# Down-projection weight sums stored unsplit, and block products added to the residual in place

## The chip, the cores and the metric

The kernel runs on one core of one Trainium2 chip. The metric is the device time of one execution in microseconds (us), the median of several runs. TensorE (PE) multiplies, VectorE (DVE) and ScalarE (ACT) do elementwise work, GpSimd (POOL) helps a little, and SyncE (SP) issues nearly all DMAs. Each engine takes its own instructions in order: an instruction that waits holds up all that stand behind it on that engine.

## The reference

A trunk of two layers over 1024 prompt frames and 32 sample frames (1056 columns), width 1024, all in float32. Layer 0 mixes by retention, layer 1 by gated linear attention (GLA); each is followed by a ConvFFN.

```python
for i in range(DEPTH):
    h = rmsnorm(x, norm_mix[i])
    y, S = retention_mixer(h, ...) if i % 2 == 0 else gla_mixer(h, ...)
    x = x + y
    h = rmsnorm(x, norm_ffn[i])
    u = h @ w_up                        # 1024 -> 2 x 2816
    c = conv_b + sum of 3 shifted u * conv_w
    gate, val = jnp.split(c, 2, axis=-1)
    x = x + (jax.nn.silu(gate) * val) @ w_down      # 2816 -> 1024
return rmsnorm(x, norm_final)
```

## The kernel before

Activations lie transposed: a tile has 128 features as its partitions and up to 1056 frames along the free axis. Every float32 operand of a matmul is split into two parts, `hi` (a cast on ScalarE, line 104) and `lo = x - hi` (a subtraction on VectorE, also line 104, in `load_w`), and a product is three matmuls: hi by hi, hi by lo, lo by hi. The raw weights land in a ring of three tiles (`raw_tile`, tag `raw`), the split ones in a ring of ten (`w_tile`).

One layer runs: the mixer; `second`, which has the gate projection (`pg`), the output projection (`Down` as `d1`, tile `pd`), which writes the residual to the DRAM tensor `scr_x`; the up projection and convolution (`ffn_up`, tile `pu`), whose 22 result tiles go to `scr_h`; and the down projection, which is the subject here.

The down projection has 22 k-tiles of 128. The first 16 are done in **pieces** (`Pieces`): two groups p of 8 k-tiles. In each p, 4 pairs q of output tiles and 2 halves s of the columns make 16 **units** (p, q, s). A unit is a 2x2 block product done with seven products instead of eight (`seven`; numbers m are 1 to 7, each product is 12 matmuls of 264 columns), in three PSUM banks. VectorE puts the bank sums together (`put`, line 1148), ScalarE copies banks out (`snap`, line 1137). The seven products need sums of weights (here S and T for each pair) and sums of activations. The activation operands of one (p, s) are made by `operands` from two staging buffers: 7 splits (cast at line 1090, subtraction at 1091) and 4 subtractions (line 1095), eleven steps that are spread over the products by `step`. The half s = 1 uses the same two staging buffers as s = 0, so its load of `scr_h` (line 1081) waits until the steps of s = 0 are done.

I call the start of the pieces, where the first operands are made while the up projection ends, the **junction**, and the place where p goes from 0 to 1 and all operands are made anew the **changeover**. There is one of each in each layer.

The weight sums are made early, in the retention stage, where VectorE and ScalarE have time: `presplit` loads two weight tiles, forms S and T on VectorE (lines 296 to 299, 128x512 each), splits each into hi and lo (ScalarE line 302, VectorE line 305) and stores four tiles to `scr_w`. A head of retention has nine chunks m; four sums are made in each head. In the pieces, `weights` loads the four split tiles (`ws`) straight into the ring of split weights, along with the plain weight g (split by `load_w`) and v.

A finished unit is stored to a DRAM tensor of its own, `scr_c`, one plane for each p. The last 6 k-tiles are the **plain rest** (`Down.run`, three chunks of 384, 384 and 288 columns). Its first chunk loads the residual `xr` from `scr_x`, and `add_more` loads both planes of `scr_c` piece by piece through the raw ring (`cx`, line 955) and adds them to `xr` on VectorE (line 957). Its weights w_down are loaded through the same raw ring into tiles `kw` and `kh`, its activations come from `scr_h` into `hh` and `hl`.

A scheduler sets the order of instructions on each engine from the program order, the free buffers and its own costs. So an edit can move instructions that it does not name.

## Time and profile before

| | |
|---|---|
| median of 3 runs | 2930.09 us (2929.4 to 2930.63) |
| profiled execution | 2926.68 us, its span 2924.9 us |
| mean granted TensorE clock | 0.988 |
| busy: TensorE / weight load / VectorE / ScalarE / GpSimd | 97% / 93% / 69% / 43% / 12% |
| moved by DMA | 414.20 MB, mean 142 GB/s |
| HBM read / written | 287.52 MB / 123.32 MB |
| stages, from the span's start | retention to about 566 us; gate, output and up projection of layer 0 to about 1395; pieces to about 1575; plain rest to about 1655; GLA to about 1960; then layer 1 in the same order, its pieces from about 2650 to 2835, its rest to the end |

The profiled execution is 3.4 us below the median, and its span is 1.8 us shorter than its time. A row of a timeline gives start, duration, engine, line and operation; in square brackets stands how long the engine was idle before it and what ended that wait. A row of the waits gives engine and line that waited, what ended it, and then the total in us, the times, and the longest. In the names, `pu` and `pd` are PSUM tiles, `AR` is one large SBUF region that holds staging buffers, unit results and residual chunks, `XA` and `XB` hold split activations.

### The profile page before, as it was taken

The page shows a single profiled execution, that of the slowest core. Times are in us where ns is not written, and L with a number is a line of the kernel's source. Part 1 is how long each engine was busy: PE and PEld are TensorE (multiplying, and loading weights), DVE is VectorE, ACT ScalarE, POOL GpSimd, SP SyncE. Part 2 cuts the span into 40 slices and gives each one's busy share as a digit, 9 for nine tenths or more (in the row PEclk, how much of TensorE's full clock was granted, in tenths as well). Part 3 has the DMA queues.
Part 4 walks back from the last instruction along what each step waited for, and adds up shares of the span by engine and source line. Part 5 has one row for each costly group of instructions (what it writes and reads, how often), then busy time and mean ns, then how long its engine had stood idle before and what let it go on. Part 6 is the DMA issues. An engine that isn't in the chain of part 4 may idle for free.

```text
span 2924.9 us, 51579 instructions
## 1 busy us (share of the span) xinstructions
PE 2835.9 (97%) x20618; PEld 2729.1 (93%) x20618; DVE 2020.9 (69%) x3307; ACT 1256.0 (43%) x2255; POOL 351.9 (12%) x564
## 2 busy tenths in 40 slices
PE   8999999999999999999898999999998999998997
PEld 8788988899999999999898989999998999998997
DVE  7756665644478877777654877774498777777548
ACT  5434342422355444444332555553254444444323
POOL 3010201000000111111000132220011111111002
PEclk9999999999999999999999999999999999999998
DMA  5544534554656122222677601114642222226675
GB/s 180 180 146 139 182 133 145 178 174 164 217 182 213 65 82 96 74 82 88 232 246 231 203 21 50 50 43 151 217 149 73 73 103 76 78 78 230 233 246 162
DMA packets 204784, 414.20 MB, mean 142 GB/s; under 512 B 25056, under 2 KB 124512, under 8 KB 204544
## 3 DMA queue, kind: packets, MB, share of 16 engines
q1 hardware_dynamic: 204000, 410.32, 41.6%
q8 instruction: 161, 2.64, 0.4%
q14 instruction: 79, 0.65, 0.1%
q10 hardware_dynamic: 544, 0.59, 0.1%
HBM read 287.52 MB, written 123.32 MB: 140 GB/s over the span
## 4 chain that ended last, share of the span: by engine, by line
PE 78%; DVE 11%; DMA 5%; ACT 3%; issue 2%; POOL 1%; DVEq 0%; SPq 0%; ACTq 0%; POOLq 0%
PE pu L1048 12%; PE pu L1043 12%; PE pu L1047 12%; PE pg L124 3%; PE pg L125 3%; PE pg L126 3%; PE pj L124 3%; PE pj L125 3%; PE pj L126 3%; PE pd L966 2%; PE pd L967 2%; PE pd L965 2%; PE psv L233 2%; PE psv L231 2%; PE psv L232 2%
## 5 line engine op out<-in xcount | busy, mean ns | idle before, releaser
L104 DVE TENSOR_TENSOR wlo<-raw,whi 128x1024 fp32r<-128x1024 f32 x164 | 208.2, 1272 | 88.7 <-ACT whi L104 77.2
L104 ACT CAST whi<-raw 128x1024 fp32r<-128x1024 f32 x164 | 171.1, 1050 | 218.7 <-issue 75.9
L1222 ACT COPY AR<-pu 128x264 f32<-128x264 f32 x264 | 99.1, 375 | 309.9 <-PE pu L1048 307.2
L124 PE MATMUL pj<-XA,whi 128*128 128x384 f32 (+1 forms) x576 | 189.8, 329 | 9.9 <-ACT whi L104 7.7
L125 PE MATMUL pj<-XA,whi 128*128 128x384 f32 (+1 forms) x576 | 188.5, 327 | 0.0
L126 PE MATMUL pj<-XA,wlo 128*128 128x384 f32 (+1 forms) x576 | 187.5, 326 | 0.9 <-DVE wlo L104 0.9
L124 PE MATMUL pg<-XA,whi 128*128 128x352 f32 x576 | 186.0, 323 | 0.0
L125 PE MATMUL pg<-XA,whi 128*128 128x352 f32 x576 | 184.6, 320 | 0.0
L126 PE MATMUL pg<-XA,wlo 128*128 128x352 f32 x576 | 184.5, 320 | 0.0
L149 POOL TENSOR_TENSOR ss<-ss,sq 128x264 f32<-128x264 f32 (+2 forms) x48 | 53.1, 1106 | 963.0 <-ACT sq L138 961.5
L966 PE MATMUL pd<-XB,whi 128*128 128x264 f32 x576 | 165.3, 288 | 3.3 <-DVE XB L935 3.1
L1244 DVE SCALAR_TENSOR_TENSOR AR<-AR,cw 128x1058 f32<-128x1058 f32 x88 | 116.0, 1320 | 72.3 <-ACT AR L1243 72.2
L967 PE MATMUL pd<-XB,wlo 128*128 128x264 f32 x576 | 164.7, 287 | 0.0
L965 PE MATMUL pd<-XB,whi 128*128 128x264 f32 x576 | 161.1, 288 | 0.0
L1048 PE MATMUL pu<-XA,wgl 128*128 128x264 f32 x528 | 150.1, 284 | 0.0
L1043 PE MATMUL pu<-XA,wgh 128*128 128x264 f32 x528 | 149.4, 283 | 0.0
L1047 PE MATMUL pu<-XA,wgh 128*128 128x264 f32 x528 | 149.3, 283 | 0.0
L1218 DVE TENSOR_TENSOR AR<-AR,pu 128x264 f32<-128x264 f32 (+2 forms) x440 | 145.5, 371 | 1.1 <-PE pu L1048 1.1
L1241 POOL COPY cst<-AR 128x2 f32<-128x2 f32 x88 | 50.6, 575 | 619.2 <-DVE AR L1218 619.2
L1195 DVE TENSOR_TENSOR wtl<-rv,wth 128x1024 fp32r<-128x1024 f32 x44 | 53.9, 1225 | 98.3 <-ACT wth L1194 97.3
L1148 DVE TENSOR_TENSOR AR<-AR,pu 128x264 f32<-128x264 f32 x128 | 53.5, 426 | 98.4 <-PE pu L1048 48.1
L124 PEld LDWEIGHTS pj<-XA,whi 128*128 128x128 f32 x576 | 109.7, 190 | 10.8 <-ACT whi L104 7.7
(414 smaller groups left out, 10508.4 us busy)
## 6 DMA issues: line engine op xcount, KB each, us to landing
ws<-scr_w SPq DMA_DIRECT2D x64, 512.0 KB, 4.4
raw<-w_ro SPq DMA_DIRECT2D x55, 512.0 KB, 3.8
rg<-w_up SPq DMA_DIRECT2D x44, 512.0 KB, 3.5
rv<-w_up SPq DMA_DIRECT2D x44, 512.0 KB, 3.4
scr_h<-AR SPq DMA_DIRECT2D x44, 512.0 KB, 2.6
AR<-scr_h SPq DMA_DIRECT2D x16, 1056.0 KB, 5.9
scr_c<-AR SPq DMA_DIRECT2D x32, 528.0 KB, 4.4
scr_w<-sp SPq DMA_DIRECT2D x32, 512.0 KB, 2.6
```

The lines of the kernel that those rows point to most:

```text
L104: ins = S.copy(hi, raw), V.tensor_tensor(lo, raw, hi.bitcast(F32), op=ALU.subtract)
L124: PE.matmul(ps, hi[:, k], rh, start=kt == 0, stop=False)
L125: PE.matmul(ps, hi[:, k], xl[:, kt, c0:c0 + n], start=False, stop=False)
L126: mm = PE.matmul(ps, lo[:, k], rh, start=False, stop=kt == KT - 1)
L965: PE.matmul(o, w[0][:, k], h[0][:, :n], start=i == 0, stop=False)
L966: PE.matmul(o, w[0][:, k], h[1][:, :n], start=False, stop=False)
L967: self.last_mm = PE.matmul(o, w[1][:, k], h[0][:, :n], start=False, stop=i == nk - 1)
L1043: mm = PE.matmul(ps, wh[:, k], x[:, 0, kt], start=m in (1, 2, 4, 5) and kt == 0, stop=False, skip_group_check=True)
L1047: PE.matmul(ps, wh[:, k], x[:, 1, kt], start=False, stop=False, skip_group_check=True)
L1048: mm = PE.matmul(ps, wl[:, k], x[:, 0, kt], start=False, stop=kt == 3, skip_group_check=True)
L1218: V.tensor_tensor(u[:, d:d + n], t[:, o:o + n], b[:, o:o + n], op=op)
L1244: V.scalar_tensor_tensor(cj, uj[:, 1:T + 3], cw[:, nt, 1:2], cj, op0=ALU.mult, op1=ALU.add)
```

## The change

There are two parts.

1. `weight_sums_out` takes the place of `presplit`. It makes S and T by the same four VectorE instructions and stores them as they are: two stores instead of four, no split. It is called in chunks m = 1 to 4 of each head instead of 0, 2, 4 and 6. In the pieces, `weights` now loads S and T with `load_w`: through the raw ring, cast on ScalarE, subtraction on VectorE.
2. `scr_c` and `add_more` are gone. A unit loads its own part of the residual from `scr_x` when it starts (`home`, into one of two buffers `res`), adds it when its seventh product is in (line 1138 after), and stores the sum back to `scr_x`. The results of units have two buffers instead of four. The plain rest loads `xr` from `scr_x` alone.

```diff
-    def presplit(l, p, q, pl):
+    def weight_sums_out(l, p, q):
...
         V.tensor_tensor(rv[:, b], rv[:, b], rg[:, a], op=ALU.subtract)
-        for j, r in enumerate((rg, rv)):
-            h = pl.tile([P, D], F32R, tag="ph_", name=f"sp{i}_{j}", bufs=2)
-            S.copy(h, r)
-            nc.sync.dma_start(scr_w[l, p, q, 2 * j], h.bitcast(F32))
-            lo = r.bitcast(F32R)
-            V.tensor_tensor(lo, r, h.bitcast(F32), op=ALU.subtract)
-            nc.sync.dma_start(scr_w[l, p, q, 2 * j + 1], r)
+        nc.sync.dma_start(scr_w[l, p, q, 0], rg)
+        nc.sync.dma_start(scr_w[l, p, q, 1], rv)
...
-                if m % 2 == 0 and m < 8:
-                    j = 4 * h + m // 2
-                    presplit(j // 8, j // 4 % 2, j % 4, rp)
+                if 1 <= m <= 4:
+                    j = 4 * h + m - 1
+                    weight_sums_out(j // 8, j // 4 % 2, j % 4)
...
-                def add_more(j):
-                    for src in self.more:
-                        t = raw_tile(f"cx{uid()}")[:, :2 * n].rearrange("p (k t) -> p k t", k=2)
-                        nc.sync.dma_start(t, src[:, 2 * j:2 * j + 2, c0:c0 + n])
-                        a = xr[:, 2 * j:2 * j + 2]
-                        V.tensor_tensor(a, a, t, op=ALU.add)
...
-            self.out = [AR[:, o:o + 4 * TH] for o in (0, 4 * TH, 8288, 8288 + 4 * TH)]
+            self.out = [AR[:, o:o + 4 * TH] for o in (0, 4 * TH)]
+            self.res = [AR[:, o:o + 4 * TH] for o in (8288, 8288 + 4 * TH)]
...
             g = load_w(io["w_dn"][self.l, p, q])
-            sums = [w_tile(f"ws{uid()}") for _ in range(4)]
+            sh, sl = load_w(scr_w[self.l, p, q, 0])
+            th, tl = load_w(scr_w[self.l, p, q, 1])
...
-            nc.sync.dma_start(sums[0].bitcast(F32), scr_w[self.l, p, q, 0])
...
+            def home(u):
+                return scr_x[:, u[1]::NPAIR, 2 * u[2] * TH:2 * (u[2] + 1) * TH]
...
-                    C[u] = self.out[units.index(u) % 4].rearrange("p (j t) -> p j t", j=2)
-                c = C[u]
+                    j = units.index(u) % 2
+                    C[u] = [x[j].rearrange("p (j t) -> p j t", j=2) for x in (self.out, self.res)]
+                    nc.sync.dma_start(C[u][1], home(u))
+                c, r = C[u]
...
                 if m == 3:
-                    nc.sync.dma_start(scr_c[p, :, q::NPAIR, 2 * s * TH:2 * (s + 1) * TH], c)
+                    V.tensor_tensor(c, c, r, op=ALU.add)
+                    nc.sync.dma_start(home(u), c)
```

Three places show how the order moves. Line numbers differ by 5 to 15 between the two kernels; the suffix of a name is only its serial number.

VectorE in the first head of retention. `pg`, `pv` are the weight tiles of the sums, `sp` their hi part, `kl`, `pl`, `vl` are lo parts that TensorE needs at once. Before:

```order
L305 TENSOR_TENSOR pg_684<-pg_684,sp_0_692 128x1024
L305 TENSOR_TENSOR pv_685<-pv_685,sp_1_697 128x1024
L104 TENSOR_TENSOR wlo_681<-raw_678,whi_680 128x1024
L333 TENSOR_TENSOR tc_653<-pj_604,cos 128x2x288
L334 TENSOR_TENSOR ts_654<-pj_604,sin 128x2x288
L450 TENSOR_TENSOR pm_705<-pss_702,rmask 128x128
L469 SCALAR_TENSOR_TENSOR kl_715<-pk_711,rcol,kh_714 128x256
L457 TENSOR_TENSOR pl_708<-pm_705,ph_707 128x128
L296 TENSOR_TENSOR pv_865<-pv_865 128x512
L297 TENSOR_TENSOR pg_864<-pv_865,pg_864 128x512
L298 TENSOR_TENSOR pg_864<-pg_864 128x512
L497 SCALAR_TENSOR_TENSOR vl_744<-psv_718,rc,vh_743 128x512
```

And now:

```order
L104 TENSOR_TENSOR wlo_681<-raw_678,whi_680 128x1024
L327 TENSOR_TENSOR tc_653<-pj_604,cos 128x2x288
L328 TENSOR_TENSOR ts_654<-pj_604,sin 128x2x288
L444 TENSOR_TENSOR pm_687<-pss_684,rmask 128x128
L463 SCALAR_TENSOR_TENSOR kl_697<-pk_693,rcol,kh_696 128x256
L451 TENSOR_TENSOR pl_690<-pm_687,ph_689 128x128
L295 TENSOR_TENSOR pv_857<-pv_857 128x512
L296 TENSOR_TENSOR pg_856<-pv_857,pg_856 128x512
L297 TENSOR_TENSOR pg_856<-pg_856 128x512
L298 TENSOR_TENSOR pv_857<-pv_857,pg_856 128x512
L444 TENSOR_TENSOR pm_767<-pss_764,rmask 128x128
L491 SCALAR_TENSOR_TENSOR vl_726<-psv_700,rc,vh_725 128x512
```

The two splits of the first sum are gone; the second sum still stands ahead of `vl`, now with all four of its instructions.

SP where the pieces of layer 0 end and the plain rest begins. `scr_c<-AR` (now `scr_x<-AR`) is the store of a unit, `raw<-w_down` a weight of the rest, `AR<-scr_h` one of its activations, `cx<-scr_c` a load of `add_more`. Before:

```order
L1152 DMA scr_c<-AR_5364 256x1x528
L276 DMA dmask<-dmask 128x128
L277 DMA lmask<-lmask 128x256
L955 DMA cx_16005<-scr_c 128x2x384
L955 DMA cx_16040<-scr_c 128x2x384
L955 DMA cx_16043<-scr_c 128x2x384
L932 DMA AR_5364<-scr_h 128x384
L102 DMA raw_16071<-w_down 128x1024
L955 DMA cx_16080<-scr_c 128x2x384
L955 DMA cx_16083<-scr_c 128x2x384
L932 DMA AR_5364<-scr_h 128x384 x3
L102 DMA raw_16111<-w_down 128x1024
```

And now, from the store of the last unit but one; `AR<-scr_x 128x8x384` is the load of `xr`:

```order
L1139 DMA scr_x<-AR_5236 256x1x528
L102 DMA raw_15995<-w_down 128x1024
L273 DMA ba<-ba 128x4
L274 DMA smask<-smask 128x384
L275 DMA dmask<-dmask 128x128
L276 DMA lmask<-lmask 128x256
L1139 DMA scr_x<-AR_5236 256x1x528
L102 DMA raw_16029<-w_down 128x1024
L102 DMA raw_16063<-w_down 128x1024
L937 DMA AR_5236<-scr_x 128x8x384
L925 DMA AR_5236<-scr_h 128x384
L102 DMA raw_16098<-w_down 128x1024
```

The first weight that the rest loads for itself (raw_16071 before, raw_15995 now) has moved from behind the last unit's store and three loads of `cx` to ahead of that store; the load of `xr`, which before stood ahead of the last two stores, now stands behind the last one.

VectorE at the changeover of layer 0, from the first split for the half s = 0. `XA<-AR,XA` is such a split, `AR<-AR 128x1056` a subtraction of operands, `AR<-AR,pu` a `put`, `wlo` a lo part of a weight. Before:

```order
L1091 TENSOR_TENSOR XA<-AR_5364,XA 128x1056
L1148 TENSOR_TENSOR AR_5364<-AR_5364,pu_14887 128x264
L104 TENSOR_TENSOR wlo_14931<-raw_14928,whi_14930 128x1024
L1148 TENSOR_TENSOR AR_5364<-AR_5364,pu_14833 128x264
L1091 TENSOR_TENSOR XA<-AR_5364,XA 128x1056 x2
L1148 TENSOR_TENSOR AR_5364<-AR_5364,pu_14947 128x264
L1095 TENSOR_TENSOR AR_5364<-AR_5364 128x1056
L1148 TENSOR_TENSOR AR_5364<-AR_5364,pu_14887 128x264
L1095 TENSOR_TENSOR AR_5364<-AR_5364 128x1056
L1091 TENSOR_TENSOR XA<-AR_5364,XA 128x1056
L1148 TENSOR_TENSOR AR_5364<-AR_5364,pu_15001 128x264
L1091 TENSOR_TENSOR XA<-AR_5364,XA 128x1056
```

And now; line 1138 is the new addition of the residual, line 1080 the subtraction of operands:

```order
L1076 TENSOR_TENSOR XA<-AR_5236,XA 128x1056
L1134 TENSOR_TENSOR AR_5236<-AR_5236,pu_14787 128x264
L104 TENSOR_TENSOR wlo_14832<-raw_14829,whi_14831 128x1024
L1134 TENSOR_TENSOR AR_5236<-AR_5236,pu_14732 128x264
L1076 TENSOR_TENSOR XA<-AR_5236,XA 128x1056
L1138 TENSOR_TENSOR AR_5236<-AR_5236 128x1056
L1076 TENSOR_TENSOR XA<-AR_5236,XA 128x1056
L1134 TENSOR_TENSOR AR_5236<-AR_5236,pu_14852 128x264
L1080 TENSOR_TENSOR AR_5236<-AR_5236 128x1056
L1134 TENSOR_TENSOR AR_5236<-AR_5236,pu_14787 128x264
L1080 TENSOR_TENSOR AR_5236<-AR_5236 128x1056
L1076 TENSOR_TENSOR XA<-AR_5236,XA 128x1056
```

From the first to the last of the seven splits and three subtractions of this half (some rows go on below these) there stood six `put` and one `wlo` among them; now there are eight `put`, three `wlo`, one lo part of v (128x512) and two additions. On SP the loads of `scr_h` into the two staging buffers for s = 1 had one load of `ws` between them; now the store of a unit stands there, which waits for that unit's addition on VectorE.

More of the change, by code (lines that the diff above doesn't have):

```diff
@@ L256, in trunk_kernel @@
     scr_w = io["scr_w"]
-    scr_c = io["scr_c"]
     ident = cp.tile([P, P], F32, tag="ident", name="ident")
@@ L901, in trunk_kernel, with __init__ @@
     class Down:
-        def __init__(self, nk, wsrc, hsrc, chunks, res, sm, keep, hold, more=()):
+        def __init__(self, nk, wsrc, hsrc, chunks, res, sm, keep, hold):
             self.nk, self.wsrc, self.hsrc, self.chunks, self.res, self.sm = nk, wsrc, hsrc, chunks, res, sm
-            self.more = more
             self.hw = max(n for _, n in chunks)
@@ L970, in run @@
                     self.load(c, kt)
-                    if self.more and i < 4:
-                        add_more(i)
                     if c == len(self.chunks) - 1 and i == nk - 3:
@@ L1103, in weights @@
             g = load_w(io["w_dn"][self.l, p, q])
-            sums = [w_tile(f"ws{uid()}") for _ in range(4)]
+            sh, sl = load_w(scr_w[self.l, p, q, 0])
+            th, tl = load_w(scr_w[self.l, p, q, 1])
             v, rv = w_tile(f"wv{uid()}"), raw_tile(f"rv{uid()}")
-            nc.sync.dma_start(sums[0].bitcast(F32), scr_w[self.l, p, q, 0])
-            nc.sync.dma_start(sums[1].bitcast(F32), scr_w[self.l, p, q, 1])
-            nc.sync.dma_start(sums[2].bitcast(F32), scr_w[self.l, p, q, 2])
-            nc.sync.dma_start(sums[3].bitcast(F32), scr_w[self.l, p, q, 3])
             nc.sync.dma_start(rv[:, b], io["w_dn"][self.l, p, q + NPAIR][:, b])
@@ L1112, in weights @@
             V.tensor_tensor(v[:, b], rv[:, b], v[:, a].bitcast(F32), op=ALU.subtract)
-            sh, sl, th, tl = sums
             self.W[p, q] = {1: (g[0][:, a], g[1][:, a]), 2: (g[0][:, b], g[1][:, b]),
@@ L1328, in second @@
         down = Down(NF - NS, lambda k: io["w_down"][l, k], lambda k: scr_h[NS + k], CM, scr_x, sm,
-                    range(NF - NS), 3, (scr_c[0], scr_c[1]))
+                    range(NF - NS), 3)
         with pool(f"xb{l}") as xbp:
@@ L1560 @@
 _SCRATCH = {"scr_or": (16, P, T), "scr_og": (8, P, T), "scr_h": (NF, P, T), "scr_x": (P, KT, T),
-            "scr_w": (2, 2, NPAIR, 4, P, D), "scr_c": (2, P, KT, T)}
+            "scr_w": (2, 2, NPAIR, 2, P, D)}
 def kernel(**inputs):
```

## The prediction

> **What bounds the kernel now.** I read the page first: TensorE is the bound, and it is nearly full.
>
> ```profile
> span 2924.9 us, 51579 instructions
> PE 2835.9 (97%) x20618; PEld 2729.1 (93%) x20618; DVE 2020.9 (69%) x3307; ACT 1256.0 (43%) x2255; POOL 351.9 (12%) x564
> ```
>
> No matmul is removed, so only TensorE's idle time (89 us in all) and the slow matmuls after a wait can be won. Next I read the busy time by stretch: two of retention, the junction of layer 0 (1395 to 1425), its changeover (1471 to 1512) and the start of its plain rest (1573 to 1606); layer 1 looks alike.
>
> ```profile
> core 0: us, PE busy (x) PEld busy (x) DVE busy (x) ACT busy (x) POOL busy (x), PEclk, DMA share, GB/s
> 60.00:195.00 135.00, 131.45 (x692) 114.29 (x691) 91.96 (x164) 55.24 (x93) 16.33 (x13) 0.99 0.44 153
> 195.00:325.00 130.00, 127.71 (x674) 110.35 (x674) 84.58 (x154) 52.53 (x90) 13.80 (x11) 1.00 0.45 155
> ...
> 1395.00:1425.00 30.00, 22.11 (x141) 20.87 (x140) 29.16 (x32) 16.19 (x18) 4.69 (x4) 0.83 0.58 196
> 1471.00:1512.00 41.00, 40.07 (x327) 39.63 (x326) 33.03 (x39) 20.43 (x29) 0.00 (x0) 1.00 0.65 219
> 1573.00:1606.00 33.00, 25.07 (x130) 23.36 (x129) 18.91 (x27) 9.47 (x15) 0.00 (x0) 0.90 0.82 259
> ```
>
> Two things are to be seen. TensorE idles where the change takes work away (3.6 and 2.3 us in retention, 7.9 us at the start of the rest). And the change puts work onto VectorE where VectorE is fullest: 29.2 of 30 us at the junction, 33 of 41 at the changeover, where TensorE now hardly waits. ScalarE is at half there, so casts that move to it hide.
>
> **Retention: minus 5.** What TensorE waits for from 60 to 566 us, from the groups by line:
>
> ```profile
> L513 PE MATMUL po<-vl,ph 128*128 128x512 f32 x32 | 13.5, 420 | 5.1 <-DVE vl L497 5.1
> L511 PE MATMUL po<-vh,ph 128*128 128x512 f32 x32 | 13.0, 406 | 2.3 <-ACT vh L496 2.1
> ```
>
> The largest of these, from the timeline: VectorE stands at the second weight sum until its load is in, and `vl` is queued behind it.
>
> ```profile
> 78.86 0.69 DVE L296 TENSOR_TENSOR pv<-pv 128x512 f32<-128x512 f32 x1 [3.58 <-DMA pv<-w_dn]
> ...
> 81.72 0.79 PE L513 MATMUL po<-vl,ph 128*128 128x512 f32 x1 [3.43 <-DVE vl L497]
> ```
>
> The load waits for a raw tile, and that for the stores of the first sum. These stores now start when the sums are made, not after the splits; what leaves that chain, per sum:
>
> ```profile
> L302 ACT CAST sp<-pg x16: 1039/1051/1057, 64.7 to 530.0; 128x1024 fp32r<-128x1024 f32 x16
> L305 DVE TENSOR_TENSOR pg<-pg,sp x16: 1209/1220/1226, 67.8 to 534.1; 128x1024 fp32r<-128x1024 f32 x16
> ```
>
> Two subtractions of 1.22 us (second row) and a cast of 1.05 make 3.5 us, as much as the wait of 3.43 us. Against that one more 0.69-us instruction of the second sum now stands ahead of `vl`. So this wait shrinks by about 2.8 us. Of the other 4.0 us (7.4 minus 3.43) I take 2.2: half of them end on ScalarE, which no longer casts sums. Bounds: minus 7.4 if all go; plus 3.4 if the sums, now one in each of four neighbouring chunks, make that wait once more.
>
> **Sums in the pieces: minus 2.9.** TensorE's waits in the pieces of layer 0, then of layer 1:
>
> ```profile
> PE pu L1043 <- ACT XA L1090: 3.9, 1, 3.9
> PE pu L1043 <- ACT AR L1137: 2.8, 1, 2.8
> PE pu L1048 <- DMA ws<-scr_w: 1.8, 3, 0.9
> ...
> PE pu L1043 <- DMA ws<-scr_w: 0.3, 1, 0.3
> ```
>
> ```profile
> PE pu L1048 <- DMA ws<-scr_w: 0.8, 2, 0.5
> ```
>
> The last three rows go: 1.8 + 0.3 + 0.8 = 2.9 us. The load waited for a split tile to come free and then took its landing; now the raw tile is loaded ahead, and after the release only a cast and a subtraction are left (1.05 + 1.22 us), so I keep all of it. Bounds: 0 to minus 2.9.
>
> **Plain rest: minus 12.** In layer 0 TensorE waits three times for `kw`, 7.9 us in sum (first row), and the first wait leaves it slow (the rows below).
>
> ```profile
> PE pd L965 <- ACT kw L104: 7.9, 3, 5.0
> ```
>
> ```profile
> 1582.83 0.33 PE L966 MATMUL pd<-hs,whi 128*128 128x384 f32 x1
> 1583.00 0.34 PE L967 MATMUL pd<-hs,wlo 128*128 128x384 f32 x1
> 1588.30 0.69 PE L965 MATMUL pd<-hh,kw 128*128 128x384 f32 x1 [4.96 <-ACT kw L104]
> ...
> 1593.24 0.38 PE L967 MATMUL pd<-hh,kw 128*128 128x384 f32 x1
> ```
>
> Starts are 0.17 us apart before the wait; after it 14 matmuls take 4.9 us instead of 2.4, which is 2.5 us more. The cause is on SP, in program order:
>
> ```profile
> 1576.11 0.53 SPq L1152 DMA_DIRECT2D scr_c<-AR  x1
> ...
> 1578.29 1.45 SPq L955 DMA_DIRECT2D cx<-scr_c  x3
> ...
> 1582.91 0.34 SPq L102 DMA_DIRECT2D raw<-w_down  x1
> ```
>
> The weight is issued at 1582.9, behind `cx` loads that hold the raw ring. Now its load stands ahead of the last unit's store at 1576, and two more follow that store at once; it is there some 7 us earlier, over the 5.0 us that it was late. So 7.9 + 2.5 = 10.4 us are at stake; I take 9.5, since the fourth weight now stands behind the load of `xr`. What is late next is `xr` itself, which waits for the store of the last unit. Landing times, medians:
>
> ```profile
> scr_c<-AR SPq DMA_DIRECT2D x32, 528.0 KB, 4.4
> ...
> AR<-scr_x SPq DMA_DIRECT2D x4, 1536.0 KB, 7.1
> ```
>
> With the new addition (1.25 us, below) that store is issued at about 1577.4, `xr` at 1582 and landed at 1589. A k-tile is 24 matmuls at 0.17 us, 4.1 us; two of them end at 1583.2, so the chunk begins at 1575, and its first result is evicted once five are through: 1596. So 7 us of slack, and the load is hidden. Layer 1 has these waits in its rest:
>
> ```profile
> PE pd L965 <- DVE rm L207: 1.9, 1, 1.9
> ...
> PE pd L965 <- ACT kw L104: 0.8, 1, 0.8
> PE pd L967 <- DVE kw L104: 0.6, 1, 0.6
> ```
>
> `kw` is earlier in the same way, and `rm` is VectorE's norm behind the additions of `add_more`. Of 3.3 us I take 2.5. Bounds for both rests: 0 to minus 13.7.
>
> **VectorE in the pieces: plus 11.** Each of the 32 units gets an addition of 128x1056, and each of the 16 weight pairs two subtractions of 128x1024. The operand subtraction has the addition's shape; the `cx` additions that go are the second row.
>
> ```profile
> L1095 DVE TENSOR_TENSOR AR<-AR x8: 1250/1253/1260, 1391.7 to 1422.7; 128x1056 f32<-128x1056 f32 x8
> ```
>
> ```profile
> L957 DVE TENSOR_TENSOR AR<-AR,cx x48: 695/951/1768, 1576.8 to 2901.6; 128x768 f32<-128x768 f32 x32, 128x576 f32<-128x576 f32 x16
> ```
>
> So the pieces gain 32 x 1.25 + 32 x 1.22 = 79 us of VectorE, the rests lose about 46, retention 39. Inside a p, a pair lasts 20 us and VectorE is mostly free: nothing on the path. At a changeover it is. Four units in 41 us bring 4 x 1.25 + 4 x 1.22 = 9.9 us to the 33.0 already there: 42.9 in 41, so at least 1.9 us is late. In the order, the operands of s = 0 now have two `wlo`, two additions, a lo part of 128x512 (0.7 us, as the instruction of that shape at 78.86) and two `put` more among them (264 columns, a quarter of the addition's, so 0.3 us or more each): 2.4 + 2.5 + 0.7 + 0.6 = 6.2 us. They themselves have time, but the staging buffers come free later, and with them the operands of s = 1, which have none:
>
> ```profile
> 1488.29 0.77 SPq L1081 DMA_DIRECT2D AR<-scr_h  x1
> ...
> 1497.92 1.26 DVE L1095 TENSOR_TENSOR AR<-AR 128x1056 f32<-128x1056 f32 x1 [1.46 <-DMA AR<-scr_h]
> ...
> 1500.92 0.28 PE L1043 MATMUL pu<-XA,whi 128*128 128x264 f32 x1
> ```
>
> The load lands 9 us after its issue; three microseconds later TensorE uses the first operand made of it. A delay of 6.2 us, less the 1.5 us of VectorE's wait that fill, would leave 4.7 us on TensorE. Products of later units, which the order now pulls forward there, take part of it; a wait of this size also slows the matmuls behind it. I take 5 for each changeover, 10 in all. Bounds for each: 0 and 9.9. At the junction the first operands have one `wlo` more and one less ahead of their last split, so I take 0.5 each, with bounds of minus 2.8 (its `snap` wait gone) and plus 4.
>
> On slowing, the junction: after a wait of 2.78 us a matmul takes 0.42 us instead of 0.28.
>
> ```profile
> 1402.95 0.28 PE L1048 MATMUL pu<-XA,ws 128*128 128x264 f32 x1
> 1406.01 0.59 PE L1043 MATMUL pu<-XA,ws 128*128 128x264 f32 x1 [2.78 <-ACT AR L1137]
> 1406.39 0.42 PE L1047 MATMUL pu<-XA,ws 128*128 128x264 f32 x1
> ```
>
> The Trainium skill ("TensorE: Matmul & The Clock Gate", What's actually happening) lets the clock fall only after an idle window of about 3.4 us. By that rule changeover waits of 2 to 3 us would cost their own length alone, an estimated 2 us less in all, and the sum would be minus 11; the row above shows slow matmuls after less, and I go by it.
>
> SP issues 80 fewer DMAs, and `scr_w` moves 16.8 MB less each way; no queue is the bound, so no time is booked. The ScalarE casts (32 x 1.05 us) leave retention and hide in the pieces.
>
> **Sum.** Minus 5, 2.9, 9.5 and 2.5, plus 10 and 1: minus 8.9 us. The profiled execution took 2926.68, so 2917.8; the median shown is 3.4 us above it: 2930.09 - 8.9 = 2921.2. I predict 2921 us.
>
> **Rivals.**
> - *VectorE takes it all back.* At junction and changeover the new subtractions stand ahead of the operand splits in full: 9.9 us for each changeover, 4 for each junction, 28 us against gains of 20: plus 8, 2938 us. It decides against the change once the four places cost over 6.5 us each on average. For it: 29 of 30 us busy, and the load behind a unit's store. Against it: TensorE's order has other products there. Chance 0.20 (slower 0.12, the same 0.08).
> - *The rest only changes its wait.* The load of `xr` and what stands behind it on SP are late, as when the chain store, load takes its slow cases, and 8 of the 12 us stay: minus 1, 2929 us. For it: the DMA share of 0.82 there. Against it: 7 us of slack. Chance 0.10 (the same 0.08, slower 0.02).
> - *The changeovers cost nothing.* Products of the next pair fill every hole, or the loads land sooner: minus 18 to minus 20, 2911 us. For it: the same scheduler's order at this changeover leaves TensorE 0.9 us idle of 41 today. Against it: 42.9 us of VectorE work in 41. The Trainium skill ("DMA: Bandwidth & Descriptors", Anatomy of one DMA) fits a transfer that GpSimd issues as 2.0 us plus its bytes over 436 GB/s; for the 1.08 MB of a staging load this is an estimated 4.5 us, and s = 1 would be 4 us earlier than I reckon, which is this case; the trace's 9 us speaks against it. Chance 0.22, faster.
>
> **How the numbers follow.** The forecast, minus 3 to minus 14 us, has 0.48 (faster 0.37, the same 0.11). 0.2% is 5.9 us, about what a measurement of this kernel can tell from no change. Sums: faster 0.37 + 0.22 = 0.59; the same 0.11 + 0.08 + 0.08 = 0.27; slower 0.14. The range runs from the full gain at 2908 (all waits of 21 to 24 us gone) to 2934, halfway into the first rival; the forecast's own is 2916 to 2927.
>
> **What would show it.** Retention: the wait for `vl` near 80 us under 1 us. Pieces: no wait for a sum's DMA; new waits of PE for XA or XB near the changeovers, 3 to 6 us each, with VectorE full. Rest: no `kw` wait near 1585, PE's chunk begun without a hole, `xr` landed 5 us or more before its first use. Wrong would be: a long wait of PE for `xr`'s eviction, or changeovers without a hole.

## The result and the profile after

| | before | after |
|---|---|---|
| median (4 runs each) | 2930.36 us (2929.4 to 2932.72) | 2905.28 us (2904.3 to 2905.55) |
| profiled execution, its span | 2926.68 us, 2924.9 us | 2905.39 us, 2903.6 us |
| ratio | | 0.9913, 95% interval 0.9895 to 0.993 |

The change makes the kernel 25 us faster by the medians and 21.3 us by the two profiled spans. The difference of 3.8 us is in the execution that was profiled before, 3.7 us below its median. The step-by-step comparison goes by the spans. Measured once more (e9 below) the same kernel gave 0.9928 (0.9906 to 0.9951). The forecast was minus 8.9 us; 2905 lies 2.7 us under the range. First the page of after:

```profile
span 2903.6 us, 51344 instructions
PE 2824.7 (97%) x20618; PEld 2721.1 (94%) x20618; DVE 2019.9 (70%) x3291; ACT 1254.2 (43%) x2255; POOL 350.7 (12%) x564
```

VectorE's total is the same within 1 us: its work has moved, and has not become less. The busy time by stretch, with the columns of before: two stretches of retention, then junction, changeover and start of the rest in layer 0. The last three begin 8 or 9 us earlier than the stretches of before, as the whole stage does.

```profile
60.00:195.00 135.00, 134.88 (x720) 118.46 (x719) 84.04 (x155) 46.04 (x83) 16.61 (x14) 1.00 0.41 137
195.00:325.00 130.00, 129.01 (x684) 111.97 (x683) 79.11 (x150) 46.04 (x83) 11.89 (x11) 1.00 0.35 117
1386.00:1416.00 30.00, 21.24 (x142) 19.84 (x141) 29.26 (x31) 17.41 (x21) 6.00 (x4) 0.83 0.60 191
1463.00:1504.00 41.00, 39.23 (x314) 38.22 (x313) 36.18 (x42) 20.75 (x29) 0.00 (x0) 1.00 0.62 209
1565.00:1598.00 33.00, 29.57 (x172) 28.51 (x171) 19.72 (x32) 16.16 (x29) 1.65 (x2) 1.00 0.88 304
```

Retention is nearly full, the rest has gained 4.5 us in 33 at full clock, the changeover has lost 0.8 us and the junction 0.9. TensorE's waits in retention and in the pieces of layer 0:

```profile
PE po L507 <- DVE vl L491: 0.9, 1, 0.9
```

```profile
PE pu L1027 <- ACT XA L1075: 6.4, 1, 6.4
PE pu L1027 <- ACT XB L1075: 2.1, 3, 1.2
PE pu L1027 <- ACT AR L1121: 1.0, 1, 1.0
PE pu L1027 <- DVE AR L1205: 0.6, 1, 0.6
PE pu L1031 <- DVE XA L1076: 0.4, 1, 0.4
```

Of 7.4 us of waits in retention 0.9 is left. No wait for a sum's load is left in the pieces. The junction has one wait of 6.4 us and a shorter one where it had 2.8 and 3.9. The changeover has 1.7 us, two of the three in the second row.

The next table has the length of each stage in us, from TensorE's first matmul of that stage to that of the next, read from the timeline. "Again" is the second profile of the changed kernel; e1 and e2 are the two parts of the change alone (below).

| stage | forecast change | before | after | again | e1 sums | e2 residual |
|---|---|---|---|---|---|---|
| start, to retention's first state product | 0 | 70.5 | 69.3 | 69.0 | 68.9 | 68.6 |
| retention | -5 | 508.4 | 499.8 | 499.8 | 500.6 | 507.5 |
| gate projection 0 | 0 | 171.8 | 171.8 | 171.8 | 171.8 | 171.8 |
| output projection 0 | 0 | 190.2 | 191.3 | 190.9 | 190.5 | 190.1 |
| up projection and pieces 0 | +3.4 | 634.1 | 635.3 | 634.1 | 633.0 | 631.8 |
| plain rest 0 | -9.5 | 97.8 | 89.4 | 89.2 | 95.1 | 90.8 |
| GLA | 0 | 320.2 | 320.1 | 320.2 | 321.2 | 320.1 |
| gate and output projection 1 | 0 | 197.9 | 197.9 | 196.3 | 198.3 | 197.0 |
| up projection and pieces 1 | +4.7 | 640.4 | 642.4 | 640.5 | 639.8 | 638.5 |
| plain rest 1, to the end | -2.5 | 93.6 | 86.4 | 86.3 | 92.9 | 86.3 |

(The forecast's sums in pieces, changeover and junction are put together per layer: -2.1 + 5 + 0.5 and -0.8 + 5 + 0.5.) Between two executions of the changed kernel a stage moves by up to 2 us, so only the retention, the rests and, by its waits, the changeover can be read one by one. In the nine other runs below whose edits leave retention as in the change it takes 499.7 to 504.3 us (e5 is the longest), and 508.4 and 507.5 where it is as before: its gain is clear, but a difference of less than 5 us in that stage is not.

The first chunk of layer 0's rest, from the timeline (SP's load of `xr`, VectorE's first eviction, TensorE's two waits):

```profile
1573.64 0.58 SPq L937 DMA_DIRECT2D AR<-scr_x  x1
...
1588.87 1.59 DVE L1393 TENSOR_TENSOR AR<-AR,pd 128x384 f32<-128x384 f32 x3 [2.27 <-PE pd L953]
...
1596.26 0.91 PE L951 MATMUL pd<-hh,whi 128*128 128x384 f32 x2 [2.92 <-DVE AR L1393]
1597.65 0.45 PE L952 MATMUL pd<-hl,whi 128*128 128x384 f32 x1 [0.49 <-DVE hl L928]
```

The eviction waited for TensorE and not for `xr`, whose load is issued 15 us earlier. TensorE's waits for `kw` are gone; what is late next is the eviction itself, 3.4 us at the chunk's end (the last two rows).

Layer 1's rest, its second half and its tail, by stretch, before and then after:

```profile
2869.00:2907.60 38.60, 36.74 (x232) 35.76 (x230) 33.85 (x49) 12.82 (x28) 4.43 (x5) 0.96 0.53 167
...
2907.60:2924.90 17.30, 4.45 (x11) 2.18 (x10) 8.86 (x13) 5.94 (x16) 4.26 (x4) 0.59 0.29 102
```

```profile
2853.40:2888.00 34.60, 34.51 (x229) 33.74 (x228) 27.73 (x40) 12.38 (x28) 4.68 (x5) 1.00 0.38 128
2888.00:2903.60 15.60, 3.23 (x10) 1.65 (x10) 8.31 (x12) 5.38 (x14) 3.94 (x4) 0.73 0.28 100
```

About the same matmuls take 34.6 us instead of 38.6, at a clock of 1.00 instead of 0.96, and the tail is some 1.6 us shorter.

### The profile page after: what moved, and what is told of

It reads as the page before. It is cut to its first block, busy times and chain, and to the rows that moved or that the text cites. A ratio compares the mean times of both kernels' runs of the same rounds, so it can differ in the third digit from the quotient of the medians.

```text
span 2903.6 us, 51344 instructions
## 1 busy us (share of the span) xinstructions
PE 2824.7 (97%) x20618; PEld 2721.1 (94%) x20618; DVE 2019.9 (70%) x3291; ACT 1254.2 (43%) x2255; POOL 350.7 (12%) x564
## 4 chain that ended last, share of the span: by engine, by line
PE 85%; DVE 8%; DMA 2%; ACT 2%; issue 1%; POOL 1%; SPq 0%; DVEq 0%; ACTq 0%; POOLq 0%
PE pu L1032 13%; PE pu L1027 13%; PE pu L1031 13%; PE pd L952 3%; PE pd L953 3%; PE pd L951 3%; PE pg L124 3%; PE pg L125 3%; PE pg L126 3%; PE pj L125 3%; PE pj L124 3%; PE pj L126 3%; PE psv L233 2%; PE psv L231 2%; PE psv L232 2%
## 5 line engine op out<-in xcount | busy, mean ns | idle before, releaser
L104 DVE TENSOR_TENSOR wlo<-raw,whi 128x1024 fp32r<-128x1024 f32 x196 | 246.3, 1259 | 126.3 <-ACT whi L104 76.3
L104 ACT CAST whi<-raw 128x1024 fp32r<-128x1024 f32 x196 | 204.3, 1048 | 286.4 <-PE pj L125 91.8
L1027 PE MATMUL pu<-XA,whi 128*128 128x264 f32 x448 | 129.3, 289 | 15.4 <-ACT XA L1075 13.5
L1031 PE MATMUL pu<-XA,whi 128*128 128x264 f32 x448 | 128.5, 288 | 0.7 <-DVE XA L1076 0.7
L1032 PE MATMUL pu<-XA,wlo 128*128 128x264 f32 x448 | 127.9, 288 | 0.0
```

What stands on the lines that cost most here:

```text
L104: ins = S.copy(hi, raw), V.tensor_tensor(lo, raw, hi.bitcast(F32), op=ALU.subtract)
L1027: mm = PE.matmul(ps, wh[:, k], x[:, 0, kt], start=m in (1, 2, 4, 5) and kt == 0, stop=False, skip_group_check=True)
L1031: PE.matmul(ps, wh[:, k], x[:, 1, kt], start=False, stop=False, skip_group_check=True)
L1032: mm = PE.matmul(ps, wl[:, k], x[:, 0, kt], start=False, stop=kt == 3, skip_group_check=True)
```

## The experiments

**The two parts alone: e1 and e2.** e1 has the hunks of `weight_sums_out` and of `weights` only, e2 those of `Pieces.run` and `add_more` only.

> The first part of the change alone: weight sums unsplit in DRAM and split on load; the units still go to their own scratch and the plain rest still adds them there. Theory A (the two parts act in separate stages): only the retention gain of 8.6 us and the 1.2 us of the start come, the pieces stay within 2 us, and the rests keep their waits for kw: about 2930 - 10 = 2920 us. Rival B (the rest's gain comes from the lighter loads of sums ahead of it, not from the cx loads that are gone): the rest of layer 0 loses most of its 7.9 us wait for kw here too, 2912 us or less.

> The second part alone: units add to the residual in place, sums still split in retention and kept as four halves. Theory A: the rests give what they gave in the whole change (8.5 and 7.2 us), the retention nothing, and the addition costs the pieces 0 to 2 us: 2930 - 15 = 2915 us. Rival B: the rests keep half of the waits and the time is 2922 us or more. The two single parts should add up: e1's and e2's gains together 25 us within 3 if A holds.

Measured: e1 0.9972 (0.9963 to 0.9981), e2 0.9945 (0.9929 to 0.9962). The reductions of 0.28% and 0.55% add up to the change's 0.72 to 0.87%. By the table e1 brings the retention and leaves the rests, e2 brings the rests and leaves the retention. TensorE's longest wait in layer 0's rest, in e1 and in e2:

```profile
PE pd L960 <- ACT kw L104: 6.3, 2, 4.7
```

```profile
PE pd L956 <- DVE AR L1402: 2.9, 1, 2.9
```

Theory A holds: the parts act in separate stages. e1's rest 0 is 2.7 us shorter than before, so a little of rival B is there. In the pieces each part alone is faster than both together, by 1 to 4 us; by the stage spread this is not sure, but the waits at the changeover go the same way: 1.0 and 1.1 us (layers 0 and 1) in e1, which has the new subtractions of weights alone, none in e2, which has the additions alone, 1.7 in both layers with the two together.

**More VectorE work in the pieces: e3, e4, e13, e14, e15.** All add additions on a residual tile that is no longer needed, so the output stays; they differ in where. The five edits in one, the conditions in words:

```diff
                     V.tensor_tensor(c, c, r, op=ALU.add)
                     nc.sync.dma_start(home(u), c)
+                    for _ in range(k):      # e3: 1, e4: 3, for every unit
+                        V.tensor_tensor(r, r, c, op=ALU.add)
+                    # e13: 2 if q in (1, 2); e14: 4 if q == 1; e15: 1 for the
+                    # units (0,2,1), (0,3,0), (0,3,1), (1,0,0); otherwise 0
```

> The changed kernel with one more VectorE addition of 128x1056 (1.25 us) per unit, on the residual tile behind the store: the output is not touched. Theory A (the prediction's: VectorE is on the path at junction and changeover): four more of them at each changeover are 5 us, of which 4 show, and about 1 at each junction: plus 8 to 12 us, 2915 us. Theory B (the changeover's end is set by when the staging loads of s = 1 land, and VectorE waits there): plus 0 to 2 us, 2906 us.

> The same with three more additions per unit, 15 us of VectorE at each changeover, where the changed kernel leaves VectorE 4.8 us idle of 41. Theory A: plus 24 to 36 us, 2935 us. Theory B: the idle 4.8 us fill and the rest shows: plus 10 at each changeover, 2925 us; if products of later units cover more, plus 5 in all.

> The changed kernel with as many extra VectorE additions as e3 (32 of 128x1056), but two each at the units of the second and third weight pair of a part, none at the first and fourth: none at the junction and the changeover. Theory A (inside a part VectorE's work is off the path, only the changeover counts): no wait at the changeover beyond the 1.7 us of the change, plus 0 to 1 us on it, 0.9925. Theory B (any added VectorE work in the pieces costs, wherever it stands): as e3, plus 9 us, 0.996.

> The changed kernel with 32 extra VectorE additions of 128x1056 as in e3, but four each at the units of the second weight pair of a part, at least 20 us away from the changeover on either side (in e13 the last two extras of the third pair still fell into the changeover, at 1467.6 and 1469.1 us). Theory A (VectorE's work costs only where the operands of the next part are made): the waits of the changeover stay at 1.7 us, plus 0 to 2 us on the changed kernel (0.9913 to 0.9935). Theory B (work anywhere in the pieces costs, since it queues ahead of the operands): 3 us or more for each changeover, plus 6 to 9 us, 0.9955.

> The changed kernel with only 8 extra additions, one each at the four units that end in each changeover. Theory A: almost all of e3's price, 4 to 5 us for each changeover, plus 8 to 10 us, 0.9955. Theory B: a quarter of e3's price, plus 2 to 3 us, 0.9935.

| run | extra additions, where | ratio (interval) | changeover waits of TensorE, layers 0 / 1 | up projection and pieces 0 / 1 |
|---|---|---|---|---|
| after, again | 0 | 0.9928 (0.9906 to 0.9951) | 1.8 / 1.7 us | 634.1 / 640.5 us |
| e14 | 32, second pair | 0.9935 (0.992 to 0.995) | 1.7 / 2.7 | 634.5 / 643.0 |
| e13 | 32, second and third pair | 0.9951 (0.9937 to 0.9964) | 4.2 / 3.9 | 637.8 / 645.3 |
| e15 | 8, changeover only | 0.997 (0.9958 to 0.9983) | 5.6 / 5.0 | 641.1 / 646.0 |
| e3 | 32, one per unit | 0.997 (0.9957 to 0.9983) | 5.0 / 5.4 | 640.5 / 646.7 |
| e4 | 96, three per unit | 1.0009 (1.0 to 1.0019) | 7.6 / 7.6 | 643.8 / 650.5 |

Eight additions at the changeovers cost as much as thirty-two spread over all units, and thirty-two away from them cost nothing that can be told. So within the pieces VectorE's added work is on the path at the changeover: theory A of e14 and e15. e3 came out as its theory A, with 5.2 and 4.2 us on the pieces. e4's pieces are 8.5 and 8.1 us longer than those of the change, nearer to its theory B (10 for each changeover) than to A; another 6.8 us came in layer 0's rest and 2.7 in GLA, which neither theory had. e13, meant to show this first, did not: two of its additions still fell into the changeover, and the expectation of 0 to 1 us was wrong. TensorE's waits at layer 0's changeover in e14, then in e15:

```profile
PE pu L1027 <- ACT XB L1075: 1.7, 2, 1.3
```

```profile
PE pu L1027 <- ACT XA L1075: 4.3, 1, 4.3
PE pu L1027 <- ACT XB L1075: 0.8, 2, 0.4
PE pu L1027 <- DVE AR L1134: 0.5, 1, 0.5
```

Why does the change itself not pay this price? The staging loads of s = 1 and the casts of what they bring, in the timeline of after, then of e15, then of e2:

```profile
1483.15 0.37 SPq L1066 DMA_DIRECT2D AR<-scr_h  x1
1488.54 0.60 SPq L1066 DMA_DIRECT2D AR<-scr_h  x1
...
1490.10 1.07 ACT L1075 CAST XA<-AR 128x1056 fp32r<-128x1056 f32 x1 [1.60 <-DMA AR<-scr_h]
1495.02 1.08 ACT L1075 CAST XB<-AR 128x1056 fp32r<-128x1056 f32 x1 [0.43 <-DMA AR<-scr_h]
```

```profile
1487.91 1.54 SPq L1066 DMA_DIRECT2D AR<-scr_h  x2
...
1494.60 1.07 ACT L1075 CAST XB<-AR 128x1056 fp32r<-128x1056 f32 x1 [1.85 <-DMA AR<-scr_h]
1498.31 1.07 ACT L1075 CAST XA<-AR 128x1056 fp32r<-128x1056 f32 x1 [2.63 <-DMA AR<-scr_h]
```

```profile
1485.85 1.16 SPq L1071 DMA_DIRECT2D AR<-scr_h  x2
...
1493.55 1.08 ACT L1080 CAST XA<-AR 128x1056 fp32r<-128x1056 f32 x1
1496.57 1.08 ACT L1080 CAST XB<-AR 128x1056 fp32r<-128x1056 f32 x1 [0.69 <-DMA AR<-scr_h]
```

`XA` is the first operand of s = 1 in program order. In the change the buffer that it is made from is free 5.4 us before the other; its load goes first and alone and is there after 6.9 us. In e15 both buffers come free together, both loads go at 1488, and this buffer's is the second of the two: `XA` can be cast only 10.4 us after the first was issued, and TensorE waits 4.3 us for it. By an estimate from these rows, 0.6 of the 4.3 us would be left if the two loads had changed places (the cast would end at 1495.7 instead of 1499.4).

That the loads go together is not what costs. In e2 they also go together, this buffer's first, and TensorE waits for no operand at the changeover; e11 and e12 are the same in this. What goes with the waits is how far TensorE's own work is when `XA`'s load goes. The table counts TensorE's matmuls since the pieces of layer 0 began (a unit has 84) and gives its waits at the changeover, without those for a sum's load:

| run | `XA`'s load issued at matmul | the other load | waits, layer 0 |
|---|---|---|---|
| before | 653 | 643 | 0 |
| e2 | 662 | 667 | 0 |
| e1 | 682 | 652 | 1.0 us |
| after | 682 | 724 | 1.7 |
| e14 | 680 | 724 | 1.7 |
| e13 | 714 | 704 | 4.2 |
| e3 | 714 | 704 | 5.0 |
| e15 | 714 | 705 | 5.6 |

Layer 1 gives the same picture. So the step between the change and e15 has two parts that the runs do not separate, when the loads go and which goes first; no run changes the order and nothing else.

**The rest: its loads or its additions. e5, e6.** The added lines are given in words; they apply to the plain rest alone.

```diff
                     self.load(c, kt)
+                    if i < 4: two loads of scr_x[:, 2*i:2*i+2, c0:c0+n] into raw tiles (e5)
+                    if i < 4: twice V.tensor_tensor(a, a, a, op=ALU.max) on xr[:, 2*i:2*i+2] (e6)
```

> The changed kernel with the plain rest's two extra loads per k-tile put back (128x2x384 from the residual into the raw ring, 24 per layer), without the additions; nothing reads them, the output is the same. Theory A (these loads hold the raw ring and the queue, so the weights come late): the waits for kw at the start of layer 0's rest are back, 6 to 8 us with the slow matmuls behind them, and about 1 to 2 us in layer 1: plus 8 to 10 us on the changed kernel's 0.9913 of the time before, 0.9945. Theory B (the additions on VectorE were what held the rest): plus 0 to 2 us, 0.992.

> The changed kernel with the plain rest's 24 additions per layer put back as VectorE instructions of the same shape on the residual tile (maximum of it with itself, so the values stay), without their loads. Theory A (VectorE has room at the rest of layer 0, less in layer 1, where rm waited behind the additions): no kw wait, 0 to 2 us in layer 0, 2 to 5 us in layer 1: plus 2 to 6 us, 0.993. Theory B (the additions are the whole loss): plus 13 to 15 us in both rests, 0.996. If e5 and e6 together give less than the 15.7 us of the two rests, the pair of both is what costs.

Measured: e5 1.0045 (1.0029 to 1.0062), its rests 104.7 and 101.6 us, 15 us over the change in each. e6 0.9963 (0.9948 to 0.9977), its rests 96.6 and 88.7, GLA 3.7 us longer. In e5 SP stands at loads of `cx` and the weight behind them is late (timeline):

```profile
1581.43 6.15 SPq L948 DMA_DIRECT2D cx<-scr_x  x2
...
1589.63 0.69 PE L956 MATMUL pd<-hh,kw 128*128 128x384 f32 x1 [8.39 <-ACT kw L104]
```

Theory A of e5 holds in its kind in layer 0; in layer 1 TensorE waits for `hh` instead, 9.0 us in two waits. The size was more than expected: the loads alone cost twice what both cost before. Why so much more stays open. e6, with 7.2 us on layer 0's rest and 2.3 on layer 1's, fits neither of its theories. It shows that the additions do it too, in another way:

```profile
1583.16 7.04 DVE L948 TENSOR_TENSOR AR<-AR 128x768 f32<-128x768 f32 x8 [2.99 <-DMA AR<-scr_x]
1590.12 0.56 DVE L928 TENSOR_TENSOR hl<-AR,hh 128x384 fp32r<-128x384 f32 x1
...
1590.73 0.64 PE L957 MATMUL pd<-hl,kw 128*128 128x384 f32 x1 [4.46 <-DVE hl L928]
```

The additions wait for `xr` on VectorE, eight in a row, and `hl`, which TensorE needs, is queued behind them. So neither the loads nor the additions could have stayed; their prices don't add.

**Retention: e7, e10, e11, e12.** e7 and e10 keep the splits but store none of them: after the two stores of the changed `weight_sums_out`,

```diff
+        for j, r in enumerate((rg, rv)):
+            h = pl.tile([P, D], F32R, tag="ph_", name=f"sp{i}_{j}", bufs=2)
+            S.copy(h, r)
+            V.tensor_tensor(h, r, h.bitcast(F32), op=ALU.subtract)
```

e7 with sums in chunks 1 to 4, e10 in 0, 2, 4 and 6 as before.

> The changed kernel with the splitting work kept in retention: each sum is still cast by ScalarE into a tile of its own and subtracted by VectorE (32 casts, 32 subtractions, the raw tile held until then), but what is stored and loaded is the unsplit sum as in the change. Theory A (the prediction's: retention waited since the raw ring came free only behind the splits, so VectorE stood at the next sum): retention goes from 500 back to 506 us or more, plus 6 to 8 us, 0.994. Rival B (the four stores per sum were what the ring waited for, and the engines' work hides): retention stays at 500 to 502 us, plus 0 to 1.5 us, 0.9915.

> As e7 (the changed kernel with the casts and subtractions of the sums kept in retention, nothing of them stored), but one sum in every second chunk as before the change, not in four chunks in a row. Theory A (the splitting work on ScalarE and VectorE is what retention waited for; e7's plus 13 us over the change came from bunching it): retention 506 to 510 us as before the change (508.4), ratio 0.994. Rival B (the number of stores counts too): retention 502 to 505 us, 0.9925. Rival C (bunching is nothing): 513 us again, 0.9955.

Measured: e7 0.9977 (0.9967 to 0.9987), retention 513.0 us; e10 0.9988 (0.9978 to 0.9997), retention 514.6. Theory A of e7 holds in its kind, at twice the size. Bunching costs nothing that can be told (rival C of e10), and the splits alone cost 13 to 15 us on the change, more than the whole gain of 8.6; why more than in the kernel before stays open. The largest wait of e10, from the timeline, stands where the one for `vl` stood before:

```profile
80.08 1.04 ACT L303 CAST sp<-pv 128x1024 fp32r<-128x1024 f32 x1
...
81.03 0.68 ACT L494 ACTIVATE vh<-psv,rc 128x512 fp32r<-128x512 f32 x1
...
81.76 0.50 PE L509 MATMUL po<-vh,ph 128*128 128x512 f32 x1 [3.63 <-ACT vh L494]
```

VectorE does not wait for a load of the sums here; `vh` is queued on ScalarE behind the cast of the sum, and TensorE waits as long as before. e11 takes e2 and makes 12 of the 16 sum pairs (split, as before) in the gate projections, 4 in retention; e12 stores these 4 unsplit and splits them on load:

```diff
         for f in range(ntile):
             w = weights(wg, f)
+            if f % 2:
+                j = f // 2 + 4 * l
+                presplit(l, j // 4, j % 4, ...)     # hi parts in free AR space
```

> Residual in place as in the change, sums stored split as before it; but 12 of the 16 pairs are formed and split in the two gate stages, where TensorE does not wait and VectorE is busy 68 of 174 us and 40 of 93, and only 4 in retention, one per head. If what the runs showed adds up: retention within 2 us of the change's 500 us, the pieces as with the residual alone (631.8 and 638.5, 3.5 and 4 us under the change), the rests as in the change: minus 5 to minus 8 us on the change, 0.989. Against it: the gate stages get 3 MB more per pair, 24 MB in 174 us of layer 0 (138 GB/s on 169): if the weights of the gate come late, TensorE waits there and the gain is gone, 0.993 or more.

> As e11, but the four pairs of layer 1 that were still split in retention (one per head) are now stored unsplit there and split on load, so retention splits nothing; the other 12 pairs are formed and split in the gate stages. If the splits alone hold retention: retention 500 us (e11 505.2), the rest of the kernel as in e11, 5 us under e11 and 3 to 6 us under the changed kernel: 0.991. Rival: the pairs' loads and stores in the gate stages delay what follows them (the first down part took 193.0 us in e11 and 191 in the change), and splits on load in layer 1's pieces cost 1 to 2 us: no better than the change, 0.9928.

Measured: e11 0.9932 (0.9911 to 0.9953), retention 505.2 with 4.9 us of waits for `vh`, the longest 3.9, pieces 633.2 and 638.9; e12 0.991 (0.9897 to 0.9924), retention 498.4 with no wait at all, pieces 633.3 and 638.6. The gate projections took 171.8 and 92.7 as ever, so moving the sums there is free in that stage; the output projection behind it took 193.0 in e11 and 190.4 in e12. e11's expectation of 0.989 was missed, by its retention. e12 against e11 gives four split pairs 6.8 us, most of the 8.6 of all sixteen. e12's interval overlaps the change's, and its span of 2898.1 us is 5.5 under the first profile of the change and equal to the second (2898.0), so it is not shown to be faster.

**The addition on GpSimd: e8.**

```diff
-                    V.tensor_tensor(c, c, r, op=ALU.add)
+                    G.tensor_tensor(c, c, r, op=ALU.add)
```

> The changed kernel with the units' residual addition on GpSimd, which does nothing in the pieces, instead of VectorE. Theory A (VectorE's 42 us of work at a changeover are one step below the point where TensorE waits, as the run with one addition more showed with 4.7 us for each changeover): little to win, since the waits left there are 1.7 us: 0 to minus 4 us, 0.990 to 0.9913. Theory B (the two halves of the change cost each other 4.6 us in the pieces of each layer, as the pieces of the single parts suggest): minus 6 to minus 9 us, 0.9885. Against both: a slow addition on GpSimd holds the last unit's store and with it the residual's load of the rest, up to plus 5 us.

Measured: 0.9991 (0.9982 to 1.0001), pieces 641.6 and 647.3, rest 94.4. Both theories fell. The addition's row in e8:

```profile
L1138 POOL TENSOR_TENSOR AR<-AR x32: 2447/2466/3582, 1422.9 to 2839.1; 128x1056 f32<-128x1056 f32 x32
```

It takes 2.47 us there and 1.25 on VectorE. The longest of TensorE's waits at the changeover:

```profile
PE pu L1027 <- DVE AR L1134: 3.2, 2, 2.0
```

They end on `put` (line 1134 now); another 1.6 us end on a `snap`, and of the waits for operands 1.0 us is left, for a split of `XA`. Why `put` is late, in the timeline:

```profile
1513.13 3.50 POOL L1138 TENSOR_TENSOR AR<-AR 128x1056 f32<-128x1056 f32 x1 [17.40 <-DVE AR L1134]
1514.24 2.94 DVE L1094 TENSOR_TENSOR wv<-rv,wv 128x512 fp32r<-128x512 f32 x1
1517.11 0.76 DVE L1134 TENSOR_TENSOR AR<-AR,pu 128x264 f32<-128x264 f32 x2
...
1517.57 0.39 PE L1027 MATMUL pu<-XB,whi 128*128 128x264 f32 x1 [1.96 <-DVE AR L1134]
```

`put` does not wait for GpSimd's result; it is queued behind the lo part of v, which takes 2.94 us here and 0.68 otherwise, and ends only after GpSimd's addition has. At 1483.05 an operand subtraction takes 3.52 us instead of 1.25 in the same way. So moving the addition away did not free VectorE at the changeover: it stood still for part of it.

**The changed kernel again: e9.**

> The changed kernel once more, unedited, beside the next two on one chip: 0.9913 of the time before, within 0.002. Its stages by the profile say how far a stage moves from run to run: retention 500 us, the pieces 635.3 and 642.4, the rests 89.4 and 86.4, each within 1 us, if the differences read so far are the kernels' own.

Measured: 0.9928 (0.9906 to 0.9951), with the stages of the first table. The pieces and the output projection of layer 1 moved by more than the 1 us expected, 1.2 to 2.

## Why the prediction was off, step by step

- *VectorE in the pieces, plus 11: this step failed.* "A delay of 6.2 us, less the 1.5 us of VectorE's wait that fill, would leave 4.7 us on TensorE ... I take 5 for each changeover". The new waits are 1.7 us in each layer, at full clock. The added work was counted nearly right (four additions and three more `wlo` in the stretch of 41 us, 8.7 us against 9.9) and so was its place (e14, e15). But the 42.9 us of VectorE in that stretch were not reached: three operand steps have moved out behind it, and VectorE is busy for 36.2. And wrong was to move both staging loads together by the sum of what is queued. The load that brings `XA` was the second of the two before and is the first now: it goes 29 matmuls later in TensorE's work, about 3.5 us and not 6.2, and is there after 6.9 us instead of 9.6. The other goes 81 matmuls later, and the longer of the two waits that are left, 1.2 us, is for an operand made after it. The order of SP, which was there to be read, has the two loads apart. The price of 5 is the right one for the next step, an addition more per unit (e3: 5.2 and 4.2 us on the pieces of the first profile of after). The junction has 0.9 and 1.0 us more of waits; as 0.9 us of waits for sums went there in layer 0, which another term books, it cost 1.7 and 1.0, forecast 0.5 each.
- *Retention, minus 5: right in kind, too small.* It gave 8.6 in both profiles. Waits of 7.4 us fell to 0.9, which is 6.5. The other 2.1 I put down to the slow matmuls behind the waits, which I counted in the rest and not here, so my bound of 7.4 was none. In the 4.3 us behind the longest wait of before the granted clock is 0.66, which is 1.5 us of them (last section). I put the wait of 3.43 us down to the late load alone. e10 has such a wait without a late load, now for `vh` behind a cast. So the splits can hold TensorE by themselves; how much of the wait before was theirs and how much the load's, no run separates.
- *Sums in pieces, minus 2.9: right.* No such wait is left.
- *Plain rest, layer 0, minus 9.5: right, 8.5 and 8.6.* The waits for `kw` and their slow stretch went, and `xr` was hidden as said; 3.4 us came back at the chunk's eviction, for which the sum had no term (I had named a wait there only for a late `xr`).
- *Plain rest, layer 1, minus 2.5: mis-sized, 7.2.* The waits of 3.3 us all went. Between its first and last matmul TensorE took 76.3 us before and takes 70.7: 5.6 us, so 2.3 beyond the waits, mostly slow matmuls (1.5 are shown in the last section), and the tail gave 1.6. I had counted the waits alone.
- *The rest of the sum.* The start gave 1.2, the output projection of layer 0 took 1.1: both are within what such stages move from run to run (start 68.6 to 71.7 us over all kernels here).

By terms the 12.4 us between minus 8.9 and minus 21.3 are 4.8 from the pieces, 4.7 from layer 1's rest, 3.6 from retention, 1.2 from the start, against 1.1 each from layer 0's rest and output projection; the small remainder is rounding and other stages. The rival nearest to what happened was "the changeovers cost nothing" with its 2911 us, by way of loads that land sooner: the two staging loads were there 6.9 and 6.5 us after their issue, before 6.5 and 9.6. That its number is so near is in part luck: the changeovers did cost 1.7 us each, and 8.3 us of the gain beyond the forecast are retention's and layer 1's rest, which the rival took as the forecast did. The Trainium skill's fit ("DMA: Bandwidth & Descriptors", Anatomy of one DMA) gave an estimated 4.5 us for such a load; no run here comes down to it.

## What to carry to other kernels

When an engine's queue gets more work ahead of a load, look in the new order which load brings the operand that is needed first, and how far the bound engine's own work is when that load goes; the sum of the queued work is not the delay. Price a wait together with the slow matmuls behind it, everywhere and not just where a row shows them at first sight: here that was 2 us in retention and 2 us in one rest. A margin that hides 10 us of new work can be used up by the next 5: measure it with dummy work put at the suspected place and away from it.

## What the runs showed of the hardware

**A wait shorter than I took slows the clock.** After the wait of 1.86 us in layer 1's rest of the kernel before, in the timeline:

```profile
2896.42 0.40 PE L965 MATMUL pd<-hh,whi 128*128 128x288 f32 x1 [1.86 <-DVE rm L207]
...
2896.93 0.29 PE L965 MATMUL pd<-hh,whi 128*128 128x288 f32 x1
2897.19 0.43 PE L967 MATMUL pd<-hh,wlo 128*128 128x288 f32 x1
...
2900.54 0.33 PE L967 MATMUL pd<-hh,kw 128*128 128x288 f32 x1
2900.71 0.30 PE L965 MATMUL pd<-hh,kw 128*128 128x288 f32 x1
```

The matmuls start at full speed, fall to 0.44 us after 0.8 us, stay there for 3.4 us (14 matmuls, 0.24 us apart instead of 0.13: 1.5 us lost) and are fast again; the granted clock from 2896.3 to 2900 is 0.62. The Trainium skill ("TensorE: Matmul & The Clock Gate", What's actually happening) says that the clock is set by windows of about 3.4 us that run freely: the length of the slow stretch agrees. That it takes an idle window of that length does not: 1.86 us of waiting was enough here, while the two waits of 0.6 and 1.2 us at the changeover of after left it at 1.00.

The stretch behind the wait of 3.43 us in retention, with the granted clock as the third number from the end:

```profile
81.70:86.00 4.30, 4.28 (x13) 3.43 (x14) 3.37 (x8) 2.37 (x4) 0.00 (x0) 0.66 0.29 122
```

**GpSimd** needs 2.47 us for an addition of 128x1056 that takes VectorE 1.25. In e8 a VectorE instruction that reads two SBUF tensors and starts while that addition runs ends 0.55 to 1.12 us after it, in all 14 cases: 3.52 us instead of 1.25 at 1483.05, 2.94 instead of 0.68 at 1514.24. `put`, which reads one of its two from PSUM, keeps its 0.43 us (at 1432.56, beside an addition from 1432.31 to 1434.79).
